# The conditioning vector of a Hymba block, spread over all partitions by eight transposes of one column each, and 24 warming matmuls where there were 31

## The chip, the cores and the metric

The kernel runs on one core of one Trainium2 chip. The metric is the device time of one execution in microseconds (us). Before the change it is 238.06 us, the median of three runs (237.94 to 239.41).

## The reference

One decoder layer for 512 tokens of width 1024, in float32. All of `x`, `c` and the weights are float32. Cut to what matters:

```python
c_act = jax.nn.silu(c)                                   # (1, 1024)
mod = c_act @ w_mod + b_mod                              # (1, 3072)
shift, scale, gate = jnp.split(mod, 3, axis=-1)
h = rmsnorm(x, norm_gain) * (1.0 + scale) + shift        # (512, 1024)
proj = h @ w_in                                          # (512, 3072)
q, k, v, z_attn, x_lru, z_lru = jnp.split(proj, splits, axis=-1)
attn = moba_attention(apply_rope(q), apply_rope(k), v)   # block-sparse causal, 8 heads x 64
y_attn = rmsnorm(attn, attn_out_gain) * silu(z_attn)
rec = rg_lru(causal_depthwise_conv(x_lru), ...)
y_lru = rmsnorm(rec, lru_out_gain) * silu(z_lru)
y = jnp.concatenate([y_attn, y_lru], axis=-1) @ w_out
return rmsnorm(x + gate * y, final_gain)
```

## The kernel before

`h` is kept transposed: eight tiles `h0` to `h7`, each of 128 channels by 512 tokens. Tile d is made from four transposes of normalised tokens (`xp`, line 412 for d >= 1, line 416 for d = 0, where they are issued one by one), and ScalarE applies the modulation to it as a scale and a bias per partition (line 419, `g`, twice: rounded as `h0h` and in full as `h`). Every matrix product is made of three passes over rounded halves (`h0h` and `h0l`, `w01h` and `w01l`, and so on): high by high, low by high, high by low. `split` (lines 233 and 251) makes the halves of a weight, the high one on ScalarE, the low one on VectorE.

The first phase accumulates seven column groups of the projection in seven PSUM banks (`acc`, line 431), d = 0 to 7, 21 matmuls of 512 columns for each d. For each d the modulation columns `shift` and `scale` have to be there: VectorE multiplies rows of the transposed `w_mod` (`ws`) by `cb`, which is SiLU(c) repeated on all 128 partitions, and sums along the row (line 384 for d = 0 in four pieces, line 396 after it). After that come the other columns, attention, the recurrence and the output product.

`cb` is made at the start. A small load brings `first`, 11 rows of 128: eight rows of c, then gain, shift and scale of d = 0. ScalarE takes SiLU of the eight rows (`crow`, line 320). TensorE turns `first` (line 325) so that VectorE can pick gain, shift and scale as columns (`v0`, line 326). Eight f32 products then spread `crow` (line 336): the stationary operand is one column of the identity repeated 128 times, over 8 rows, so each product repeats one row of `crow` on 128 partitions. They fill two banks `cp`, which are copied to `cb` (line 234).

TensorE's queue at the start also carries `NWARM` matmuls of 512 columns over a constant tile `warm` into a bank `spare` nobody reads (line 312).

The order of instructions on every engine comes from a planner (`Plan.emit`): each operation has a cost and a due time, the planner places the operation that can start first by its own model, and among those that can start within 0.12 us the one that is due first. The due times and costs are the numbers in `op(...)`. The engines execute their own queue in the order in which it was emitted. A load is issued on SyncE's queue (line 240).

Of the kernel before, what the change touches and what calls it, by code (L numbers as in the profile page):

```python
# [10 lines left out]
AF = mybir.ActivationFunctionType  # L11
OP = mybir.AluOpType
# [5 lines left out]
ND = D // 128  # L18
# [1 line left out]
BIG = 3.0e38  # L20
LRU_C = 8.0
NFIRST = 7
NWARM = 31
CUTS = (((0, 768), (768, 1024)), ((0, 512), (512, 1024)))
REST = (14.6, 14.7, 17.2, 17.3)

# [34 lines left out]
class Plan:  # L61
# [11 lines left out]
    def op(self, eng, cost, fn, r=(), w=(), due=None, table=None, lat=0.25, after=0.0, alt=None):  # L73
        o = Op(eng, cost, fn, list(r), list(w), due, table, lat, after, alt)
        deps = set()
        for b in o.r:
            if b.writer is not None:
                deps.add(b.writer)
        for b in o.w:
            if b.writer is not None:  # L80
                deps.add(b.writer)
            deps.update(b.readers)
        for b in o.r:
            b.readers.append(o)
        for b in o.w:
            b.writer, b.readers = o, []
        for b in set(o.r) | set(o.w):
            b.users += 1
        deps.discard(o)
        o.deps = list(deps)  # L90
        for d in deps:
            d.outs.append(o)
        o.left = len(deps)
        self.ops.append(o)
        return o
# [82 lines left out]
def tile_hymba_block(ctx: ExitStack, tc: tile.TileContext, x, ws0, wss, wgt, win0, wv, winr,  # L178
                     wo, wg, vecs, top, fgain, consts, out):
    nc = tc.nc  # L180
    V, A, G, PE, SP = nc.vector, nc.scalar, nc.gpsimd, nc.tensor, nc.sync
# [19 lines left out]
    op = plan.op  # L201
# [4 lines left out]
    def t4(name, dt=F32, shape=(128, 1024)):  # L206
        return Buf("t4", list(shape), dt, name)

    def bank(name, kind=None):
        return Buf("ps", [128, 512], F32, name, kind)  # L210

    def col(name):
        return Buf("c", [128, 2], F32, name)

    def fix(name, shape, dt=F32):
        return Buf("fix", list(shape), dt, name)


    def dv(n, ptr=0):
        return 0.075 + n / 960.0 + 0.06 * ptr  # L220
# [10 lines left out]
    def copy(n, dst, src, r, w, due=None, psum=False, after=0.0):  # L231

        op("A", acp(n) if psum else ac(n), lambda: A.copy(dst(), src()), r, w, due, after=after,  # L233
           alt=("V", dv(n) if psum else dv2(n), lambda: V.tensor_copy(dst(), src())))
# [27 lines left out]
    def t_first(d):  # L262
        return T_FIRST + 4.79 * d
# [10 lines left out]
    vec, ident, cst = fix("vec", [128, NV]), fix("ident", [128, 128]), fix("cst", [128, 2048])  # L274
    first = fix("first", [11, 128])
# [34 lines left out]
    op("V", 0.3, lambda: V.memset(warm[:], 1.0), [], [warm], -10)  # L310
    for n in range(NWARM):
        op("PE", 0.32 if n < 11 else 0.235, lambda: PE.matmul(spare[:], warm[:, 0:128], warm[:], start=True, stop=True),  # L312
           [warm], [spare], 5.3 + 0.28 * n, lat=0.0)


    epsc, ones, junk, crow = fix("epsc", [128, 1]), fix("ones", [128, 1]), fix("junk", [128, 1]), fix("crow", [ND, 128])
    op("V", 0.1, lambda: V.memset(epsc[:], EPS), [], [epsc], -20)
    op("V", 0.1, lambda: V.memset(ones[:], 1.0), [], [ones], 0)
    op("A", 0.1, lambda: A.activation(junk[:], epsc[:], AF.Silu), [epsc], [junk], -6, "silu")
    op("A", 0.1, lambda: A.activation(crow[:], first[0:ND, :], AF.Silu), [first, junk], [crow], -5, "silu")  # L320
    op("A", 0.1, lambda: A.activation(junk[:], epsc[:], AF.Sqrt), [epsc, crow], [junk], -4, "sqrt")


    ps, v0 = bank("v0"), fix("v0", [128, 3])
    op("PE", 0.2, lambda ps=ps: PE.transpose(ps[:, 0:11], first[:], ident[0:11, 0:11]), [first, ident], [ps], 1)
    op("V", 0.2, lambda ps=ps: (V.tensor_copy(v0[:, 0:2], ps[:, ND:ND + 2]), V.tensor_scalar(
        v0[:, 2:3], ps[:, ND + 2:ND + 3], 1.0, None, op0=OP.add)), [ps], [v0], 2)
    cb = t4("cb")
    for half in range(2):
        ps = bank("cp")  # L330
        s = slice(half * 512, (half + 1) * 512)

        def spread(ps=ps, half=half):
            for j in range(4):
                k = half * 4 + j
                PE.matmul(ps[:, j * 128:(j + 1) * 128], ident[0:ND, k:k + 1].to_broadcast([ND, 128]), crow[:], start=True, stop=True)  # L336
        op("PE", 0.8, spread, [crow, ident], [ps], 2)
        copy(512, lambda s=s: cb[:, s], lambda ps=ps: ps[:], [ps], [cb], 4.5 + 0.5 * half, True)


# [3 lines left out]
    for t in range(NT):  # L344
# [8 lines left out]
        for dst, cut, e, due2, after in ((xs[t], slice(0, 256), "VVAA"[t], due + 0.4, 0.0), (xt[t], slice(256, D), "A", 20.0 + t, REST[t])):  # L353
# [5 lines left out]
            else:  # L359
# [9 lines left out]
                                         op0=OP.add), [vec], [vec], t_first(1) - 3)  # L369

    sch = col("sch")

    def part(d, j):
        return ws[d][j][:, j] if d >= 4 else ws[d][j][:]

    def gain(d):

        sc, g = col("sc"), col("g")
        half = (sc, sch)
        for j in (1, 0):  # L380
            if d == 0:
                for n in range(2):
                    lo, up = CUTS[j][n]
                    op("V", dv(up - lo), lambda j=j, n=n, lo=lo, up=up: V.scalar_tensor_tensor(
                        ws[0][j][n][:], ws[0][j][n][:], 1.0, cb[:, lo:up], op0=OP.mult, op1=OP.mult,
                        accum_out=half[n][:, j:j + 1]), [ws[0][j][n], cb], [ws[0][j][n], half[n]], 8 - 2 * j + 0.7 * n)
                    if j and not n:
                        op("V", 0.1, lambda: V.tensor_add(sc[:, 1:2], sc[:, 1:2], v0[:, 2:3]), [sc, v0], [sc], 9.2)
                if j:
                    op("V", 0.2, lambda: V.tensor_scalar(g[:, 1:2], sch[:, 1:2], sc[:, 1:2], v0[:, 0:1],  # L390
                                                         op0=OP.add, op1=OP.mult), [sc, sch, v0], [g], 9.4)
                else:
                    op("V", 0.15, lambda: V.scalar_tensor_tensor(g[:, 0:1], sc[:, 0:1], v0[:, 1:2], sch[:, 0:1],
                                                                    op0=OP.add, op1=OP.add), [sc, sch, v0], [g], 9.5)
                continue
            op("V", dv(1024), lambda j=j: V.scalar_tensor_tensor(  # L396
                part(d, j), part(d, j), 1.0, cb[:], op0=OP.mult, op1=OP.mult, accum_out=sc[:, j:j + 1]),
               [ws[d][j], cb], [ws[d][j], sc])
        if d == 0:
            return g  # L400
        op("V", 0.2, lambda: V.tensor_scalar(
            g[:, 1:2], sc[:, 1:2], vec[:, V_SCALE + d:V_SCALE + d + 1], vec[:, V_GAIN + d:V_GAIN + d + 1],
            op0=OP.add, op1=OP.mult), [sc, vec], [g])
        op("V", 0.1, lambda: V.tensor_add(g[:, 0:1], sc[:, 0:1], vec[:, V_SHIFT + d:V_SHIFT + d + 1]), [sc, vec], [g])
        return g

    for d in range(ND):
        g, xp = gain(d), bank(f"xp{d}")
# [18 lines left out]
        for i, (a, b) in enumerate(((0, hh[d]), (1, hh[d]), (0, hl[d]))):  # L427
            for j in range(NFIRST):
                w, k = wp[j // 4][a], j if d else j % 4
# [293 lines left out]
    for u, name in enumerate(UNITS):  # L723
        kind, idx = name[0], int(name[1])
        t1 = t_step(8 * (u + 1))
        ps = unit(u)
# [41 lines left out]
    for g in range(4):  # L768
# [12 lines left out]
        for t in range(NT):  # L781
# [3 lines left out]
            for n, (lo, up) in enumerate(zip(cuts, cuts[1:])):  # L785
                ps, w = bank("po"), up - lo
# [39 lines left out]
                for to, up, mark in ((outa[t], 512, done_a), (outb[t], 512, done_b))[:1 if last else 2]:  # L826
                    fns = dict(A=lambda t=t, to=to, up=up: A.activation(to[:, :up], to[:, :up], AF.Copy, scale=ssq[t][:, 3:4]),
                               V=lambda t=t, to=to, up=up: V.tensor_scalar(to[:, :up], to[:, :up], ssq[t][:, 3:4], None, op0=OP.mult))
# [86 lines left out]
```

## Time and profile before

| | us |
|---|---|
| median of three runs | 238.06 |
| lowest and highest | 237.94, 239.41 |
| the profiled execution | 238.57 |
| its span, first to last instruction | 236.5 |
| TensorE busy in the span | 229.0 |
| VectorE busy | 203.8 |
| ScalarE busy | 139.3 |

The profile is of one execution; its times count from the first instruction. Engines: PE is TensorE's matmuls, PEld its weight loads, which overlap the matmuls, DVE is VectorE, ACT is ScalarE, SP is SyncE, which here only issues loads and stores. A busy share is an average over the program; which engine sets the end is read from the chain of work that ended last and from what each engine waited for.

### The profile page before, as it was taken

What the parts mean: (1) busy time and instruction counts of PE and PEld (TensorE: products, weight loads), DVE (VectorE), ACT (ScalarE), POOL (GpSimd) and SP (SyncE); (2) the same over time, 40 slices, a digit from 0 to 9 for tenths busy, and PEclk for the clock granted to TensorE, in tenths of its full rate; (3) what the DMA queues carried; (4) which work ended last, traced back from release to release, by engine and by line L of the source; (5) the groups of instructions that cost most, each with busy time, mean ns of one, the idle gap of its engine ahead of it and who ended that gap; (6) DMA issues with size and microseconds to landing.
All of it is one profiled execution on the core that took longest, in us unless ns stands there. A gap on an engine that the chain in (4) does not pass through costs nothing.

```text
span 236.5 us, 3435 instructions
## 1 busy us (share of the span) xinstructions
PE 229.0 (97%) x1236; PEld 181.2 (77%) x1236; DVE 203.8 (86%) x396; ACT 139.3 (59%) x263; POOL 9.5 (4%) x32
## 2 busy tenths in 40 slices
PE   7999999999999999999999999999999999999990
PEld 5457888888888788786788887878887788888890
DVE  1679998895999899899999999989998999956583
ACT  7859464652659587799992347766374711303363
POOL 1010000057000000000000000000000000000000
PEclk9999999999999999999999999999999999999997
DMA  6999999822045223755122354474521000000044
GB/s 232 378 418 417 416 418 423 327 91 89 11 169 177 89 89 103 256 191 167 61 118 89 92 190 180 166 256 190 177 89 65 26 0 3 0 0 0 0 180 177
DMA packets 11782, 38.54 MB, mean 163 GB/s; under 512 B 1515, under 2 KB 1782, under 8 KB 11638
## 3 DMA queue, kind: packets, MB, share of 16 engines
q1 hardware_dynamic: 11600, 38.06, 43.5%
q10 hardware_dynamic: 166, 0.27, 0.3%
q8 instruction: 10, 0.16, 0.3%
q14 instruction: 6, 0.05, 0.1%
HBM read 36.22 MB, written 2.10 MB: 162 GB/s over the span
## 4 chain that ended last, share of the span: by engine, by line
PE 96%; ACT 1%; DVE 1%; issue 0%
PE acc L431 17%; PE pj L243 14%; PE pj L245 13%; PE pj L244 13%; PE po L243 6%; PE po L245 6%; PE po L244 6%; PE spare L312 4%; PE av L616 4%; PE sc L570 4%; PE tp L633 4%; PE cp L336 2%; PE xp L412 1%; PE ss L758 1%; PE gi L243 0%; PE gi L245 0%
## 5 line engine op out<-in xcount | busy, mean ns | idle before, releaser
L586 ACT ACTIVATE z<-z,mn 128x128 f32<-128x128 f32 (+3 forms) x32 | 17.7, 554 | 7.9 <-DVE mn L583 7.2
L396 DVE SCALAR_TENSOR_TENSOR ws<-ws,cb 128x1024 f32<-128x1024 f32 x14 | 16.9, 1219 | 0.4 <-DMA ws<-in_wss_dram 0.4
L583 DVE CUSTOM_DVE_ANT_0 z<-sc,cst 128x128 f32<-128x128 f32 (+3 forms) x32 | 14.2, 487 | 1.6 <-PE sc L570 1.6
L233 ACT COPY pt<-tp 128x128 f32<-128x128 f32 (+3 forms) x26 | 8.5, 391 | 6.2 <-PE tp L633 6.2
L312 PE MATMUL spare<-warm 128*128 128x512 bf16 x31 | 10.2, 486 | 1.5 <-DVE warm L310 1.5
L796 DVE SCALAR_TENSOR_TENSOR xr<-po,rba,xr 128x512 f32<-128x512 f32 (+2 forms) x9 | 6.2, 692 | 6.2 <-PE po L245 6.0
L807 ACT ACTIVATE o<-xr 128x512 f32<-128x512 f32 x7 | 4.4, 635 | 12.0 <-DVE xr L796 12.0
L633 PE MATMUL tp<-ident,z 128*128 128x128 f32 x80 | 10.5, 272 | 0.0
L633 PEld LDWEIGHTS tp<-ident,z 128*128 128x128 f32 x80 | 9.4, 140 | 1.4
L778 DVE TENSOR_TENSOR wo<-wo,grow 128x1024 f32<-128x1024 f32 x8 | 9.8, 1219 | 0.0
L541 DVE SCALAR_TENSOR_TENSOR wgt<-wgt,cb 128x1024 f32<-128x1024 f32 x8 | 9.7, 1218 | 0.0
L495 DVE SCALAR_TENSOR_TENSOR xc<-xl,vec,xc 128x511 f32<-128x511 f32 (+2 forms) x12 | 9.0, 747 | 0.2
L616 PE MATMUL av<-pt,v 128*64 128x512 f32 (+3 forms) x64 | 9.1, 436 | 0.0
L312 PEld LDWEIGHTS <-warm 128*128 128x128 bf16 x31 | 3.5, 118 | 6.1 <-issue 2.9
L616 PEld LDWEIGHTS av<-pt,v 128*64 128x64 f32 x64 | 4.3, 137 | 5.0 <-issue 4.1
L598 DVE TENSOR_SCALAR z<-z,sum 128x384 f32<-128x384 f32 (+3 forms) x20 | 7.2, 387 | 0.4
L233 ACT CAST wo21h<-wo 128x1024 fp32r<-128x1024 f32 x1 | 1.1, 1054 | 9.7 <-DVE wo L778 9.7
L657 ACT ACTIVATE sz<-pj 128x512 f32<-128x512 f32 x8 | 4.8, 599 | 3.3 <-PE pj L245 2.8
L419 ACT ACTIVATE h<-xp,g 128x512 f32<-128x512 f32 x8 | 6.2, 771 | 0.0
L597 ACT ACTIVATE z<-z,sum 128x128 f32<-128x128 f32 (+3 forms) x12 | 6.2, 546 | 0.0
L796 DVE SCALAR_TENSOR_TENSOR xr<-po,rbl,xr 128x512 f32<-128x512 f32 x8 | 6.0, 747 | 0.2
L586 ACT ACTIVATION_READ_ACCUMULATOR z<-z,mn 128x1 f32 x32 | 6.0, 188 | 0.0
(1121 smaller groups left out, 753.5 us busy)
## 6 DMA issues: line engine op xcount, KB each, us to landing
wc<-in_winr_dram SPq DMA_DIRECT2D x13, 512.0 KB, 3.3
ws<-in_wss_dram SPq DMA_DIRECT2D x4, 1024.0 KB, 11.1
wgt<-in_wgt_dram SPq DMA_DIRECT2D x8, 512.0 KB, 3.3
wo<-in_wo_dram SPq DMA_DIRECT2D x8, 512.0 KB, 3.4
w<-in_win_dram SPq DMA_DIRECT2D x7, 448.0 KB, 8.8
ws<-in_wss_dram SPq DMA_DIRECT2D x6, 512.0 KB, 6.4
x<-in_x_dram SPq DMA_DIRECT2D x4, 512.0 KB, 5.4
wv<-in_wv_dram SPq DMA_DIRECT2D x4, 512.0 KB, 3.8
```

The costliest lines, as they stand in the source:

```text
L243: PE.matmul(ps, lh, rh, start=start, stop=False)
L244: PE.matmul(ps, lh, rl, start=False, stop=False)
L245: PE.matmul(ps, ll, rh, start=False, stop=stop)
L312: op("PE", 0.32 if n < 11 else 0.235, lambda: PE.matmul(spare[:], warm[:, 0:128], warm[:], start=True, stop=True), [warm], [spare], 5.3 + ...
L396: op("V", dv(1024), lambda j=j: V.scalar_tensor_tensor(part(d, j), part(d, j), 1.0, cb[:], op0=OP.mult, op1=OP.mult, accum_out=sc[:, j:j + ...
L431: PE.matmul(acc[j][:], w[:, k * 128:(k + 1) * 128], b[:], start=first, stop=last),
L583: op("V", dv(n) + 0.085, lambda s=s, z=z, mn=mn: V.tensor_tensor_reduce(out=z[:, :n], in0=ps[s][:, cut], in1=cst[:, 2048 - n:2048], op0=OP ...
L586: op("A", ac(n, 1, 1), lambda s=s, z=z, mn=mn, sm=sm: A.activation(z[:, :n], z[:, :n], AF.Exp, bias=mn[:, 0:1], scale=-1.0, accum_out=sm[: ...
L616: PE.matmul(pss[u][64 * s:64 * s + 64, k * 128:], vt[k][:, h * 64:h * 64 + 64], pts[2 * u + s][:, k, k * 128:], start=(k == 0), stop=(k == 3))
L633: PE.transpose(at(h)[:, k * 128:(k + 1) * 128], z[:, k * 128:(k + 1) * 128], ident[:])
L778: op("V", dv(1024), lambda w=w, s=s: V.tensor_mul(w[:], w[:], grow[:, None, s].to_broadcast([128, 2, 512])), [w, grow], [w], t0 - 7 + 2 * j)
L796: op("V", dv(w, 1), lambda t=t, ps=ps, c0=c0, c1=c1, br=br: V.scalar_tensor_tensor(res[t][:, c0:c1], ps[:, :c1 - c0], rb[br][:, t:t + 1], ...
```

## The change

SiLU is written back into `first`. The turn of `first` then carries the eight activated rows of c as well, all eleven columns are copied to `v0`, and eight transposes spread columns 0 to 7 of `v0`: the operand that is turned is one column repeated 128 times. The tile `crow` goes, the added 1 of the scale column gets a tile `one`, and the gain and shift columns of `v0` move behind the eight of c. `NWARM` becomes 24.

```diff
-NWARM = 31
+NWARM = 24
...
-    op("A", 0.1, lambda: A.activation(crow[:], first[0:ND, :], AF.Silu), [first, junk], [crow], -5, "silu")
-    op("A", 0.1, lambda: A.activation(junk[:], epsc[:], AF.Sqrt), [epsc, crow], [junk], -4, "sqrt")
+    op("A", 0.1, lambda: A.activation(first[0:ND, :], first[0:ND, :], AF.Silu), [first, junk], [first], -5, "silu")
+    op("A", 0.1, lambda: A.activation(junk[:], epsc[:], AF.Sqrt), [epsc, first], [junk], -4, "sqrt")
...
-    ps, v0 = bank("v0"), fix("v0", [128, 3])
-    op("PE", 0.2, lambda ps=ps: PE.transpose(ps[:, 0:11], first[:], ident[0:11, 0:11]), [first, ident], [ps], 1)
-    op("V", 0.2, lambda ps=ps: (V.tensor_copy(v0[:, 0:2], ps[:, ND:ND + 2]), V.tensor_scalar(
-        v0[:, 2:3], ps[:, ND + 2:ND + 3], 1.0, None, op0=OP.add)), [ps], [v0], 2)
+    ps, v0 = bank("v0"), fix("v0", [128, ND + 3])
+    op("PE", 0.3, lambda ps=ps: PE.transpose(ps[:, 0:ND + 3], first[:], ident[0:ND + 3, 0:ND + 3]), [first, ident], [ps], 1)
+    op("V", 0.15, lambda ps=ps: V.tensor_copy(v0[:], ps[:, 0:ND + 3]), [ps], [v0], 2)
+    one = fix("one", [128, 1])
+    op("V", 0.1, lambda: V.tensor_scalar(one[:], v0[:, ND + 2:ND + 3], 1.0, None, op0=OP.add), [v0], [one], 3)
...
-                PE.matmul(ps[:, j * 128:(j + 1) * 128], ident[0:ND, k:k + 1].to_broadcast([ND, 128]), crow[:], start=True, stop=True)
-        op("PE", 0.8, spread, [crow, ident], [ps], 2)
+                PE.transpose(ps[:, j * 128:(j + 1) * 128], v0[:, k:k + 1].to_broadcast([128, 128]), ident[:])
+        op("PE", 0.85, spread, [v0, ident], [ps], 2.5)
```

On TensorE, at the start of the program before the change: `v` is the turned `first`, `cp` the spread, `warm` and `spare` the warming matmuls.

```order
L312 LDWEIGHTS warm
L312 MATMUL spare<-warm 128x512
L325 MATMUL v_101<-ident,first 128x11
L336 MATMUL cp<-crow,ident 128x128 x8
L312 LDWEIGHTS warm
L312 MATMUL spare<-warm 128x512
```

The same place after the change:

```order
L312 LDWEIGHTS warm
L312 MATMUL spare<-warm 128x512
L325 MATMUL v_102<-ident,first 128x11
L312 LDWEIGHTS warm
L312 MATMUL spare<-warm 128x512
L312 LDWEIGHTS warm
L312 MATMUL spare<-warm 128x512
L337 MATMUL cp<-ident,v_105 128x128 x8
L312 LDWEIGHTS warm
L312 MATMUL spare<-warm 128x512
```

Ahead of the turn stand five warming matmuls where there were four, between the turn and the spread two where there was none, and between the spread and the first transpose of `xs` six where there were eight. Between the first and the second transpose of `xs` there are five where there were seven.

On TensorE, from the third transpose of `xs` (line 416 before, 417 after) to the first accumulation, before the change; behind the second transpose and ahead of the first row here stand nine warming matmuls:

```order
L416 MATMUL xp_145<-ident,xs_188 128x128
L312 LDWEIGHTS warm
L312 MATMUL spare<-warm 128x512
L312 LDWEIGHTS warm
L312 MATMUL spare<-warm 128x512
L312 LDWEIGHTS warm
L312 MATMUL spare<-warm 128x512
L416 MATMUL xp_145<-ident,xs_198 128x128
L412 MATMUL xp_208<-ident,xs_134 128x128
```

After the change, with six warming matmuls ahead of the first row that is shown as a transpose:

```order
L312 LDWEIGHTS warm
L312 MATMUL spare<-warm 128x512
L417 MATMUL xp_148<-ident,xs_186 128x128
L417 MATMUL xp_148<-ident,xs_193 128x128
L413 MATMUL xp_201<-ident,xs_138 128x128
L413 MATMUL xp_201<-ident,xs_157 128x128
```

The three warming matmuls between the last two transposes of `xs` are gone, and of the nine ahead of them six are left. On the other engines no instruction changes its place.

## Rows read from the trace of the kernel before

**Rows 1.** The page: busy time of each engine with its share of the span, and the chain of work that ended last, by engine.

```profile
PE 229.0 (97%) x1236; PEld 181.2 (77%) x1236; DVE 203.8 (86%) x396; ACT 139.3 (59%) x263; POOL 9.5 (4%) x32
PE 96%; ACT 1%; DVE 1%; issue 0%
```

**Rows 2.** The chain of work that ended last in order of time, 0 to 25 us: start, duration, engine, tile written, line, instructions merged.

```profile
3.63 3.61 PE cp L336 x16
7.24 3.52 PE spare L312 x8
10.77 0.21 PE xp L416
10.98 1.73 PE spare L312 x7
...
12.82 1.94 PE spare L312 x9
14.76 0.11 PE xp L416
14.87 0.65 PE spare L312 x3
...
15.66 0.79 ACT h0h L419
...
16.49 6.96 PE acc L431 x28
```

**Rows 3.** ScalarE's timeline, 10 to 22 us: start, duration, engine, line, operation, tile written and read, and in brackets the idle time before it and what ended it.

```profile
11.03 1.08 ACT L357 ACTIVATE xs<-x,ss 128x256 f32<-128x256 f32 x2
12.73 0.62 ACT L233 CAST w00512h<-w 128x512 fp32r<-128x512 f32 x1 [0.62 <-DMA w<-in_win_dram]
15.66 0.78 ACT L419 ACTIVATE h0h<-xp,g 128x512 fp32r<-128x512 f32 x1 [2.31 <-PE xp L416]
16.34 0.50 ACT L233 CAST w00384h<-w 128x384 fp32r<-128x384 f32 x1
...
19.07 0.93 ACT L233 CAST w01h<-w 128x896 fp32r<-128x896 f32 x1
...
20.74 0.77 ACT L419 ACTIVATE h1h<-xp,g 128x512 fp32r<-128x512 f32 x1
```

**Rows 4.** VectorE's timeline, 3 to 20 us, with the same columns.

```profile
3.67 0.16 DVE L326 COPY v<-v 128x2 f32<-128x2 f32 x1 [2.18 <-PE v L325]
...
7.28 0.69 DVE L234 COPY cb<-cp 128x512 f32<-128x512 f32 x1 [1.01 <-PE cp L336]
...
10.16 0.69 DVE L384 SCALAR_TENSOR_TENSOR ws<-ws,cb 128x512 f32<-128x512 f32 x1 [0.20 <-DMA ws<-in_ws_dram]
...
13.19 0.22 DVE L393 SCALAR_TENSOR_TENSOR g<-sc,v,sch 128x1 f32<-128x1 f32 x1
...
14.52 1.23 DVE L396 SCALAR_TENSOR_TENSOR ws<-ws,cb 128x1024 f32<-128x1024 f32 x1 [0.44 <-DMA ws<-in_wss_dram]
...
16.87 0.56 DVE L251 TENSOR_TENSOR w00384l<-w,w00384h 128x384 fp32r<-128x384 f32 x1 [1.12 <-ACT w00384h L233]
17.35 1.22 DVE L396 SCALAR_TENSOR_TENSOR ws<-ws,cb 128x1024 f32<-128x1024 f32 x1
...
18.49 0.69 DVE L421 TENSOR_TENSOR h0l<-h,h0h 128x512 fp32r<-128x512 f32 x1
...
19.50 0.15 DVE L404 TENSOR_TENSOR g<-sc,vec 128x1 f32<-128x1 f32 x1
```

**Rows 5.** Issues of single loads on SyncE's queue (duration of the issue in ns, smallest, median and largest, and first and last start in us) and the time from issue to landing: the two pieces of the weights of d = 0, the weights of d = 1 (`w01`), the second half of `ws` of d = 1.

```profile
L240 SPq DMA_DIRECT2D w<-in_win_dram x2: 527/797/1067, 4.6 to 5.7; - x2
DMA to landing us min/median/max: 7.5/7.8/8.1
L240 SPq DMA_DIRECT2D w<-in_win_dram x1: 328/328/328, 10.8 to 10.8; - x1
DMA to landing us min/median/max: 6.2/6.2/6.2
L240 SPq DMA_DIRECT2D ws<-in_wss_dram x1: 327/327/327, 10.2 to 10.2; - x1
DMA to landing us min/median/max: 5.7/5.7/5.7
```

**Rows 6.** TensorE's timeline, 16.4 to 22 us: the first products of `h0l` and of `h1h`.

```profile
16.49 1.21 PE L431 MATMUL acc<-h0h,w00512h 128*128 128x512 f32 x4 [0.43 <-ACT h0h L419]
...
19.83 1.07 PE L431 MATMUL acc<-h0l,w00512h 128*128 128x512 f32 x4
...
21.56 0.73 PE L431 MATMUL acc<-h1h,w01h 128*128 128x512 f32 x2
```

**Rows 7.** Who waited for whom: the only two rows of TensorE's matmuls over the whole program, then one of ScalarE from 14 to 62 us (us in total, times, longest).

```profile
PE spare L312 <- DVE warm L310: 1.5, 1, 1.5
PE acc L431 <- ACT h0h L419: 0.4, 1, 0.4
ACT h3h L419 <- PE xp L412: 2.5, 1, 2.5
```

**Rows 8.** The chain in order of time, one row of 176 to 182 us (`tp` are transposes of the attention), and the last 3.3 us of the span by stretch: length, busy time and instructions of PE, PEld, DVE, ACT and POOL, the granted clock as a share of 2.4 GHz, DMA share and GB/s.

```profile
177.80 1.75 PE tp L633 x16
233.20:236.50 3.30, 0.00 (x0) 0.00 (x0) 0.00 (x0) 0.00 (x0) 0.00 (x0) 0.50 0.46 176
```

More of the change, by code (lines that the diff above doesn't have):

```diff
@@ L313, in tile_hymba_block @@
            [warm], [spare], 5.3 + 0.28 * n, lat=0.0)
-    epsc, ones, junk, crow = fix("epsc", [128, 1]), fix("ones", [128, 1]), fix("junk", [128, 1]), fix("crow", [ND, 128])
+    epsc, ones, junk = fix("epsc", [128, 1]), fix("ones", [128, 1]), fix("junk", [128, 1])
     op("V", 0.1, lambda: V.memset(epsc[:], EPS), [], [epsc], -20)
@@ L387, in gain @@
                     if j and not n:
-                        op("V", 0.1, lambda: V.tensor_add(sc[:, 1:2], sc[:, 1:2], v0[:, 2:3]), [sc, v0], [sc], 9.2)
+                        op("V", 0.1, lambda: V.tensor_add(sc[:, 1:2], sc[:, 1:2], one[:]), [sc, one], [sc], 9.2)
                 if j:
-                    op("V", 0.2, lambda: V.tensor_scalar(g[:, 1:2], sch[:, 1:2], sc[:, 1:2], v0[:, 0:1],
+                    op("V", 0.2, lambda: V.tensor_scalar(g[:, 1:2], sch[:, 1:2], sc[:, 1:2], v0[:, ND:ND + 1],
                                                          op0=OP.add, op1=OP.mult), [sc, sch, v0], [g], 9.4)
                 else:
-                    op("V", 0.15, lambda: V.scalar_tensor_tensor(g[:, 0:1], sc[:, 0:1], v0[:, 1:2], sch[:, 0:1],
+                    op("V", 0.15, lambda: V.scalar_tensor_tensor(g[:, 0:1], sc[:, 0:1], v0[:, ND + 1:ND + 2], sch[:, 0:1],
                                                                     op0=OP.add, op1=OP.add), [sc, sch, v0], [g], 9.5)
```

## Prediction

> **What bounds the kernel now.** I read the totals first. TensorE is busy for 229.0 of 236.5 us, and the chain of work that ended last runs over it for 96% of the span [rows 1], so a change counts only if it lets TensorE reach its useful matmuls sooner or do fewer of them. Then the chain in order of time. Up to 15.6 us it names nothing but TensorE, and none of that is a product of the layer: 16 passes of the eight `cp` products, then 8, 7, 9 and 3 warming matmuls with the four transposes of `xs` between them [rows 2]. The first accumulation starts at 16.49 and from there the chain is TensorE again. The list of waits says that this stays so: over the whole program TensorE's matmuls wait twice, 1.5 us for `warm` at the start and 0.4 us for `h0h` [rows 7]. So the end of the kernel follows the start of the accumulations, d = 0 at 16.49 and d = 1 at 21.56 [rows 6].
>
> What does the first one wait for? In ScalarE's timeline `h0h` starts at 15.66 after 2.31 us of idle time that ended with a transpose of `xs` on TensorE [rows 3]. Its other inputs were there earlier: `g` is written at 13.19 + 0.22 = 13.41 [rows 4], and both late `xs` tiles by 11.03 + 1.08 = 12.11 [rows 3]. TensorE works strictly in its order, and the transposes of those two tiles stood behind nine and three warming matmuls. That is 2.2 us in which everything else was ready.
>
> **The clock in these rows.** Eight warming matmuls of 512 columns take 3.52 us from 7.24 (0.44 each, the 1.2 GHz level), nine take 1.94 from 12.82 (0.215 each, the 2.4 GHz level). The seven from 10.98 take 1.73, which is one slow and six fast: the clock rose near 11.4 [rows 2]. A transpose of 128 columns takes 0.21 before and 0.11 after [rows 2].
>
> **Part 1, the spreading of c.** Removed: eight f32 products, 3.61 us on TensorE [rows 2]. Added: eight transposes. At the low clock I take the 0.21 of the transpose at 10.77 for each, 1.7 us in all. Nothing shows a transpose whose stationary operand is one column repeated; the bound above is the price of the removed product, 3.61 / 8 = 0.45 each, the bound below the fast 0.11. I stay with 0.21, the row of the same operation at the same clock. Three more warming matmuls now stand ahead (one before the turn of `first`, two behind it), 3 x 0.44 = 1.3. So the last `cp` ends at 7.24 + 1.3 - 3.6 + 1.7 = 6.6 instead of 7.24.
>
> The change adds a wait: the transposes need `v0`, which VectorE copies out of PSUM after the turn; the same copy took 0.16 us from 3.67 [rows 4]. Behind the waiting transposes stand all the warming matmuls and the `xs` transposes. The two warming matmuls between turn and spread, 0.88 us, cover the copy; without that cover it would cost some 0.3. Who needs the result is `cb`, whose second half is copied at 7.28 and would now be at some 6.7; its first reader starts only at 10.16, and waited for a DMA then [rows 4]. Even at the upper bound (`cp` ending at 8.5, `cb` at 9.3) this reader sees nothing. So part 1 by itself is worth nothing at VectorE; what it gives is 0.6 us of TensorE's queue. The other edits (SiLU in place, one wider copy instead of two small ones, the added one in a tile of its own) are single short instructions with margin of the same kind, and I cost them at nothing.
>
> **Part 2, seven warming matmuls fewer.** The order shows where: none remains behind the second `xs` transpose but six, and none between the third and the fourth. From 6.6: six at 0.44 end at 9.3, the first `xs` transpose at 9.5, five more (four of them slow, if the clock again rises near 11.4) at 11.55, the second transpose at 11.65, six fast ones at 12.95, the last two transposes at 13.2. They need `xs` of 12.11, so they wait for nothing. `h0h` then starts at the latest of 13.2 (transposes), 13.41 (`g`) and the end of the `w00512h` cast, 12.73 + 0.62 = 13.35 [rows 3], so near 13.45: **2.2 us** sooner. If the clock rises 2 us later than that, some 1.3 us come on top for TensorE and `h0h` starts near 14.5.
>
> **What is late next.** Each engine's queue behind `h0h` has to come 2.2 sooner too, or it gives back time.
> - ScalarE: the cast of `w00384h` follows `h0h` by 0.68, so 14.13; its load landed 7.5 to 8.1 after issues at 4.6 and 5.7 [rows 5], 13.2 at the latest. No stall.
> - VectorE: `w00384l` waited 1.12 for that cast [rows 4]. This wait goes, but not more: the reduction ahead of it began at 14.5, when its load came. So everything behind it on VectorE moves by 1.12 and not by 2.2: the next reduction from 17.35 to 16.23 (its load, issued at 10.2, landed 5.7 later at 15.9 [rows 5], just in time), and `h0l` from 18.49 to 17.37, ready at 18.06.
> - TensorE: the 14 products of `h0h` take 19.83 - 16.49 = 3.34 [rows 6]. From 14.27 they end at 17.6, and the products of `h0l` wait for 18.1. That is **0.45 given back**. The seven `h0l` products then take 1.6 (0.23 each, as 6.96 / 28 less the start [rows 2]) and end at 19.7.
> - d = 1: `h1h` needs `g`, which moves by 1.12 from 19.65 to 18.53 [rows 4], and ScalarE, where the cast of `w01h` moves from 19.07 to 17.0: there the load stops it, issued at 10.8 and landed 6.2 later [rows 3, 5]. Everything behind it moves by 2.07, so `h1h` starts at 18.67 and ends at 19.45, before TensorE is free at 19.7. Before, TensorE had waited about 0.1 for it.
>
> So d = 1 starts at 19.7 to 19.8 instead of 21.56: 2.2 - 0.45 + 0.1 = **1.8 us sooner**. Behind that TensorE is dense, and the others wait for it: already `h3h` stood 2.5 us for TensorE's transposes [rows 7], more than the 1.8. I find nothing that returns the 1.8.
>
> **The sum.** The profiled execution took 238.57 us, its span 236.5 and 2.1 around it; that is 0.5 over the median of 238.06. It becomes 238.57 - 1.8 = 236.8, and by the same difference the median becomes **236.3 us**, a ratio of 0.992. About 1% (2.4 us) is what a measurement of this kernel tells from no change, so the likeliest outcome lies inside it.
>
> **Rivals.**
> *The clock falls in the new gap.* In the stretch from 12.95 to 14.27 TensorE would have six transposes and then nothing, where before it had a 1 us stretch of that kind. Price: at 0.44 a product instead of 0.23, a clock that stays low for T us from 14.27 delays d = 1 by 0.47 T. The wait for `h0l` hides the first 0.45 of that and the 1.8 goes next, so from T = 2.25 / 0.47, about 5 us, on the kernel is slower than before; low through all of d = 0 (21 x 0.43 = 9 us) puts d = 1 at 23.3, 1.7 later than now: 239.8. Against it: 16 transposes alone from 177.80 took 1.75 us, 0.109 each, so the clock stood high through them; for it: it is at 0.50 in the last stretch, where TensorE has nothing at all [rows 8]. The Trainium skill (TensorE: Matmul & The Clock Gate, Part 4: PE-mode transpose) says that the full clock "doesn't engage for transpose-mode"; by that the six transposes would not count against this rival, and its 239.8 would be the sum. The row at 177.80 differs from the page: transposes there ran at the full clock and alone for longer than this gap, so the chance stays small. 0.07.
>
> *The loads become the bound.* `w01` has 0.1 us of margin and the second reduction 0.4. Every us that these land later than in this trace is a us less gained: 0.6 to 1.2 later gives 237 to 237.5. 0.15.
>
> *The change does not do what it says.* If `g` rather than the warming matmuls had set `h0h` in most executions, or the spread came after 10.16, nothing would move: 238.1. The 2.31 us row speaks against the first, a margin of 2.8 us against the second. 0.05.
>
> *More than forecast.* The kernel before carries some 18 warming matmuls behind the rise of its clock; where it rises 1 us later than in this trace, two more run slow and `h0h` comes 0.5 later. If that is the usual case the gain is 2.3 or more: 235.7. 0.10.
>
> **How the numbers follow.** The forecast has 0.63, with 235.9 to 236.8 as its own range (0.1 to 0.5 us for the landings, and as much for the clock's moment). The range of 8 in 10 leaves out the falling clock and the lower part of the last rival, 0.12 or so, and with the edges of the forecast not above 2 in 10; it takes in the late loads and no change, with 0.1 for the spread of a median: 235.4 to 238.2. Faster by over 1% (below 235.7) is only the better half of the last rival and the edge of the forecast: 0.09. Slower by over 1% needs a clock that stays low into d = 1, 10.5 us: 0.04. Within 1%: 0.87.
>
> **What would show it.** Right: `h0h` starts near 13.45 after a wait for `g`, not for TensorE; eight `cp` transposes of 0.21; TensorE waits about 0.4 for `h0l`; d = 1 starts near 19.75, and the span ends 1.8 sooner with everything behind d = 1 unchanged in spacing. Wrong: products of `h0h` 0.43 apart instead of 0.23 (clock), an idle stretch of ScalarE ahead of `w01h` that ended with a DMA (loads), or `h0h` still behind `xs` transposes.

## The result, and the profile after

| | before | after |
|---|---|---|
| median of 20 runs, us | 238.57 | 236.77 |
| lowest and highest | 237.84, 239.44 | 235.79, 239.01 |
| profiled execution, its span | 238.57, 236.5 | 237.26, 235.2 |
| d = 1 starts in the profile | 21.56 | 20.38 |

The ratio is 0.9929 with a 95% interval of 0.991 to 0.9948: 1.8 us faster, the size that was forecast, inside the 1% that was named. The profile after shows that this number came about in another way than the working said.

TensorE's timeline after, 4 to 21 us, with the columns of [rows 6]:

```profile
4.82 1.91 PE L337 MATMUL cp<-ident,v 128*128 128x128 f32 x8
6.53 1.77 PE L312 MATMUL spare<-warm 128*128 128x512 bf16 x6
...
8.25 1.24 PE L312 MATMUL spare<-warm 128*128 128x512 bf16 x5
...
9.43 1.46 PE L312 MATMUL spare<-warm 128*128 128x512 bf16 x6
...
11.70 0.33 PE L417 MATMUL xp<-ident,xs 128*128 128x128 f32 x1 [0.36 <-ACT xs L358]
...
13.88 2.00 PE L432 MATMUL acc<-h0h,w00512h 128*128 128x512 f32 x4 [1.41 <-ACT h0h L420]
15.68 1.49 PE L432 MATMUL acc<-h0h,w00384h 128*128 128x512 f32 x3
16.95 1.30 PE L432 MATMUL acc<-h0h,w00512l 128*128 128x512 f32 x4
...
18.79 1.07 PE L432 MATMUL acc<-h0l,w00512h 128*128 128x512 f32 x4
...
20.38 0.84 PE L432 MATMUL acc<-h1h,w01h 128*128 128x512 f32 x3
```

The eight transposes of the spread start at 4.82 and the next matmul at 6.53, 0.21 each. Of the six warming matmuls behind them the most, and all behind those, run at 0.215: the clock rose near 7 us, where before it rose near 11.4 [rows 2]. The trace's own record of the granted clock begins with this rise, at 7.15 us after and at 11.30 before. The clock column of a stretch (third from the end, with the columns of [rows 8]) counts nothing ahead of the record and reads 1.00 there, as in this stretch of the profile before, in which the warming matmuls take 0.44. So ahead of the first rise the level is read from the spacing of the matmuls.

```profile
5.90:11.80 5.90, 5.90 (x20) 2.95 (x19) 3.67 (x14) 4.83 (x12) 0.00 (x0) 1.00 1.00 377
```

After the change TensorE is therefore through with its 24 warming matmuls at 11 us, waits 0.36 us for `xs`, and after the transposes stands empty for 1.41 us until `h0h` is there. Then the first seven products of `h0h` are 0.45 and 0.42 apart instead of 0.23: the clock has fallen. By the trace's record it is at 0.50 from 13.98 to 17.39. Stretches of the profile after, with the same columns:

```profile
14.20:16.80 2.60, 2.60 (x7) 2.04 (x7) 2.60 (x4) 2.42 (x5) 1.08 (x1) 0.50 1.03 408
17.50:20.00 2.50, 2.50 (x13) 2.04 (x12) 2.46 (x6) 2.50 (x5) 0.00 (x0) 1.00 1.02 406
```

ScalarE's timeline after, which answers [rows 3]:

```profile
12.37 0.62 ACT L233 CAST w00512h<-w 128x512 fp32r<-128x512 f32 x1 [0.72 <-DMA w<-in_win_dram]
13.05 0.78 ACT L420 ACTIVATE h0h<-xp,g 128x512 fp32r<-128x512 f32 x1
13.73 0.50 ACT L233 CAST w00384h<-w 128x384 fp32r<-128x384 f32 x1
...
16.73 0.94 ACT L233 CAST w01h<-w 128x896 fp32r<-128x896 f32 x1 [0.18 <-DMA w<-in_win_dram]
...
18.42 0.76 ACT L420 ACTIVATE h1h<-xp,g 128x512 fp32r<-128x512 f32 x1
```

`h0h` starts 2.6 us sooner and directly behind the cast of `w00512h`, whose load ends the wait; the transposes of `xs` no longer hold it. VectorE's first reduction waits for a DMA, as before, and it has `h0l` at 16.96 + 0.69:

```profile
9.66 0.69 DVE L385 SCALAR_TENSOR_TENSOR ws<-ws,cb 128x512 f32<-128x512 f32 x1 [0.26 <-DMA ws<-in_ws_dram]
...
12.73 0.22 DVE L394 SCALAR_TENSOR_TENSOR g<-sc,v,sch 128x1 f32<-128x1 f32 x1
...
16.96 0.69 DVE L422 TENSOR_TENSOR h0l<-h,h0h 128x512 fp32r<-128x512 f32 x1
```

TensorE reaches the products of `h0l` only at 18.79, a us after that, since it runs slowly; d = 1 starts 1.2 us sooner than before, and the span ends 1.3 sooner. This profile is not the usual case. The other runs have no trace, but each has its mean granted clock, and a fall of 3.4 us to half takes 0.007 from the mean over 235 us. In 8 of the 20 runs the mean is 0.983 to 0.988 (0.987 in the profiled one) and the time 237.1 to 239.0, median 237.5; in the other 12 it is 0.991 to 0.998 and the time 235.8 to 237.0, median 236.5. That the first group are the runs in which the clock fell is read from these means. The means also hold a low stretch at the end of the span, which every profile has, so a single run near the border could be misplaced. The median of all lies within the faster group.

### The profile page after: what moved, and what is told of

Same layout as the page of the kernel before. It is cut to its first block, busy times and chain, and to the rows that moved or that the text cites. A ratio compares the mean times of both kernels' runs of the same rounds, so it can differ in the third digit from the quotient of the medians.

```text
span 235.2 us, 3405 instructions
## 1 busy us (share of the span) xinstructions
PE 226.1 (96%) x1221; PEld 179.7 (76%) x1221; DVE 203.9 (87%) x396; ACT 139.7 (59%) x263; POOL 9.5 (4%) x32
## 4 chain that ended last, share of the span: by engine, by line
PE 91%; DMA 3%; SPq 2%; ACT 1%; DVE 1%; issue 0%; ACTq 0%
PE acc L432 17%; PE pj L243 14%; PE pj L245 13%; PE pj L244 13%; PE po L243 6%; PE po L245 6%; PE po L244 6%; PE av L617 4%; PE sc L571 4%; PE tp L634 4%; DMA w<-in_win_dram 3%; SPq L240 2%; PE xp L413 1%; PE ss L759 1%; PE gi L245 0%; PE gi L243 0%
## 5 line engine op out<-in xcount | busy, mean ns | idle before, releaser
L312 PE MATMUL spare<-warm 128*128 128x512 bf16 x24 | 7.7, 466 | 1.5 <-DVE ones L318 1.5
L312 PEld LDWEIGHTS <-warm 128*128 128x128 bf16 x24 | 2.5, 114 | 4.1 <-DVE ones L318 1.5
```

## The experiments

The theory after the profile: products over 8 rows had kept TensorE's clock low; with the transposes it rises some 4 us sooner, that by itself sets `h0h` free, and the seven missing warming matmuls then leave TensorE empty, so that the clock falls in part of the runs. The rival is the prediction's own working: the clock rises when it did, part 1 is worth 0.6 us of queue, and the gain is that of part 2. All medians below are compared with the kernel before on the same chip: 239.02 us (17 runs) for e1 to e4, 239.01 (16 runs) for e5 and e6.

**e1: part 1 alone.** The changed kernel with

```diff
-NWARM = 24
+NWARM = 31
```

> Part 1 alone: the spread by eight transposes, 31 warming matmuls. Theory (from the profile after): with transposes in place of the products over 8 rows the clock rises near 7 us and not near 11.4, so the 18 warming matmuls behind the spread run at 0.215 and the last xs transpose comes at 12.2 to 12.5; h0h starts at 13.0 to 13.5, held by g and the w00512h cast, and TensorE is not empty before it, so the clock does not fall. Time about 1.7 us below before, ratio 0.992 to 0.994. Rival (the prediction's own working): the clock rises near 11.4 as before and part 1 gives 0.6 us of TensorE's queue; h0h near 15.0, ratio 0.997 to 0.998.

Measured: 236.06 us, six runs from 235.62 to 236.16, ratio 0.9885 (0.9862 to 0.9908). The gain of part 1 alone, 3.0 us, is larger than the theory said and larger than that of the whole change. TensorE's timeline:

```profile
6.52 1.88 PE L312 MATMUL spare<-warm 128*128 128x512 bf16 x6
...
9.54 2.10 PE L312 MATMUL spare<-warm 128*128 128x512 bf16 x9
...
12.23 0.27 PE L417 MATMUL xp<-ident,xs 128*128 128x128 f32 x1
...
13.57 1.19 PE L432 MATMUL acc<-h0h,w00512h 128*128 128x512 f32 x4 [0.41 <-ACT h0h L420]
14.60 0.84 PE L432 MATMUL acc<-h0h,w00384h 128*128 128x512 f32 x3
15.28 1.07 PE L432 MATMUL acc<-h0h,w00512l 128*128 128x512 f32 x4
...
17.43 1.19 PE L432 MATMUL acc<-h0l,w00512h 128*128 128x512 f32 x4 [0.40 <-DVE h0l L422]
...
19.15 0.86 PE L432 MATMUL acc<-h1h,w01h 128*128 128x512 f32 x3
```

The nine warming matmuls and the three behind them are there (part 2 takes six of these twelve away), but they run at 0.215, and the last transpose of `xs` comes at 12.23 and not, as in the profile before, at 15.35:

```profile
15.35 0.27 PE L416 MATMUL xp<-ident,xs 128*128 128x128 f32 x1
```

The clock rose at 7.36 by the trace's record. ScalarE starts `h0h` at 12.74, behind the cast, as in the changed kernel:

```profile
12.09 0.62 ACT L233 CAST w00512h<-w 128x512 fp32r<-128x512 f32 x1 [0.74 <-DMA w<-in_win_dram]
12.74 0.78 ACT L420 ACTIVATE h0h<-xp,g 128x512 fp32r<-128x512 f32 x1
```

TensorE waits 0.41 for it, and its first seven products come out 0.26 and 0.23 apart. The rival's clock near 11.4 and its ratio of 0.997 fall. Part of why the gain is larger than the theory said is the load behind the cast: the cast starts at 12.09 where it started at 12.73 before. Over the eight profiles of this case that start lies between 11.56 (e5) and 12.90 (e4, the changed kernel again), and no run shows whether the change has a share in it. The wait of 0.40 for `h0l` is the 0.45 that the prediction gave back.

**e2: part 2 alone.** The kernel before with

```diff
-NWARM = 31
+NWARM = 24
```

> Part 2 alone: the f32 products over 8 rows, 24 warming matmuls. Theory: the products keep the clock low, it rises near 11 us, the seven missing warming matmuls let the xs transposes end near 14.1, h0h starts near 14.15, 1.5 us sooner than before; TensorE is never empty, so the clock stays high; h0l again takes some back, ratio 0.993 to 0.995. Rival: the gain of the whole change comes from the spread alone and the count of warming matmuls does nothing: ratio 0.998 to 1.002.

Measured: 237.51 us, 12 runs from 236.84 to 239.12, ratio 0.995 (0.993 to 0.9969), 1.5 us. TensorE's timeline:

```profile
7.25 3.59 PE L312 MATMUL spare<-warm 128*128 128x512 bf16 x8
...
10.84 1.76 PE L312 MATMUL spare<-warm 128*128 128x512 bf16 x7
...
13.63 0.38 PE L416 MATMUL xp<-ident,xs 128*128 128x128 f32 x2
...
14.88 1.21 PE L431 MATMUL acc<-h0h,w00512h 128*128 128x512 f32 x4 [0.43 <-ACT h0h L419]
...
19.95 0.97 PE L431 MATMUL acc<-h1h,w01h 128*128 128x512 f32 x3
```

With the products over 8 rows the clock again rises only near 11 (eight at 0.42 from 7.25, then seven in 1.6; 11.02 by the trace's record), and `h0h` starts at 14.05, 1.6 us sooner than before:

```profile
14.05 0.78 ACT L419 ACTIVATE h0h<-xp,g 128x512 fp32r<-128x512 f32 x1 [0.74 <-DVE w00512l L251]
```

The view puts this wait down to a subtraction on VectorE that is no input of `h0h`; the last two transposes of `xs`, which are, end at the same time (13.63 + 0.38). So here the warming matmuls do stand in the way, as the working had it. TensorE is never empty for longer than 0.43 before the products of `h0h`, and the clock holds. The two parts do not add: 3.0 and 1.5 alone, 2.3 together (e4).

**e3: the gap filled.** The changed kernel with six more warming matmuls behind the fourth transpose of `xs`; the order of everything else is the same.

```diff
+NHOLD = 6
...
+        for n in range(NHOLD if not d else 0):
+            op("PE", 0.235, lambda: PE.matmul(spare[:], warm[:, 0:128], warm[:], start=True, stop=True),
+               [warm, xs[3]], [spare], 11.0 + 0.01 * n, lat=0.0)
```

> The changed kernel with six more warming matmuls behind the fourth xs transpose, where TensorE had been empty for 1.4 us before the products of h0h. Theory: the clock no longer falls during d = 0, products of h0h are 0.23 apart, every run is as fast as those of the changed kernel in which the clock held; span 234.0 to 234.7, median 0.3 to 0.6 us below the changed kernel, ratio 0.989 to 0.991. Rival: the low stretch costs nothing, since h0l waits anyway, and the runs spread for another reason: ratio 0.992 to 0.994, the same as the changed kernel.

Measured: 236.09 us, six runs from 235.64 to 236.69, ratio 0.9891 (0.9869 to 0.9913), and mean clocks of 0.991 to 0.998 in all of them. TensorE's timeline, then the stretch at the products of `h0h`:

```profile
11.56 1.46 PE L421 MATMUL spare<-warm 128*128 128x512 bf16 x6
...
13.57 1.19 PE L436 MATMUL acc<-h0h,w00512h 128*128 128x512 f32 x4
...
19.14 0.86 PE L436 MATMUL acc<-h1h,w01h 128*128 128x512 f32 x3
```

```profile
14.20:16.80 2.60, 2.60 (x13) 2.01 (x11) 2.60 (x6) 2.42 (x4) 1.01 (x1) 1.00 1.03 411
```

Thirteen matmul records in the stretch in which the changed kernel has seven, at the full clock. With work added that nobody reads, the median is 0.6 us below that of the changed kernel on the same chip (e4), and the times above 237 are gone. The intervals of e3 and e4 overlap, so the 0.6 by itself is not clear of noise; what speaks for the fillers is that the 12 runs of e1 and e3 have no mean below 0.991, where 11 of the 26 runs of the changed kernel (8 of 20 above, 3 of 6 in e4) have 0.988 or less.

**e4: the changed kernel again**, without an edit.

> The changed kernel again, for a second profile and its times beside the three others on the same chip. Ratio 0.992 to 0.994. If the clock holds in this profile: h0h near 13.1 to 13.5, TensorE waits 0.3 to 0.5 us for h0l, d = 1 starts near 19.7, span near 234.5. If it falls: d = 1 near 20.4, span near 235.2.

Measured: 236.68 us, six runs from 235.85 to 237.72, ratio 0.9917 (0.9888 to 0.9946). The clock fell in three of the six (mean 0.986 to 0.988; 237.2 to 237.7) and held in three (0.991 to 0.996; 235.9 to 236.2). The profile is again one in which it fell, this time with everything half a us later, and d = 1 at 20.88. A profile of the changed kernel with the clock held is therefore missing; e1 and e3 stand in for it.

**e5: the same products over 128 rows.** The kernel before, all 31 warming matmuls; `crow` is padded with 120 rows of zeros, the products are otherwise the same.

```diff
-    epsc, ones, junk, crow = fix("epsc", [128, 1]), fix("ones", [128, 1]), fix("junk", [128, 1]), fix("crow", [ND, 128])
+    epsc, ones, junk, crow = fix("epsc", [128, 1]), fix("ones", [128, 1]), fix("junk", [128, 1]), fix("crow", [128, 128])
...
-    op("A", 0.1, lambda: A.activation(crow[:], first[0:ND, :], AF.Silu), [first, junk], [crow], -5, "silu")
+    op("V", 0.1, lambda: V.memset(crow[:], 0.0), [], [crow], -15)
+    op("A", 0.1, lambda: A.activation(crow[0:ND, :], first[0:ND, :], AF.Silu), [first, junk, crow], [crow], -5, "silu")
...
-                PE.matmul(ps[:, j * 128:(j + 1) * 128], ident[0:ND, k:k + 1].to_broadcast([ND, 128]), crow[:], start=True, stop=True)
+                PE.matmul(ps[:, j * 128:(j + 1) * 128], ident[:, k:k + 1].to_broadcast([128, 128]), crow[:], start=True, stop=True)
```

> The kernel before with one thing changed: the same eight f32 products, but over 128 rows (crow padded with zero rows) in place of 8. They take as long as before (0.45 each, 3.6 us in all). Theory: it was the products over 8 rows that kept the clock low until 11.3; over 128 rows the clock rises near 7 to 8 us, the warming matmuls behind them run at 0.215, the last xs transpose comes near 13.4 and h0h near 13.5, with no transposes in the spread and all 31 warming matmuls; time 236.2 to 236.8, ratio 0.989 to 0.993. Rival: f32 products keep the clock low whatever their rows, or the early rise comes from the transposes themselves: the clock rises near 11.3 and the time is that of before, ratio 0.998 to 1.002.

Measured: 236.34 us, six runs from 236.05 to 236.7, ratio 0.9889 (0.9865 to 0.9912). One warming matmul moved, from ahead of the first transpose of `xs` to behind the last. TensorE's timeline:

```profile
3.70 3.63 PE L337 MATMUL cp<-crow,ident 128*128 128x128 f32 x16
7.17 1.67 PE L312 MATMUL spare<-warm 128*128 128x512 bf16 x7
8.68 0.27 PE L417 MATMUL xp<-ident,xs 128*128 128x128 f32 x1
...
13.11 0.27 PE L417 MATMUL xp<-ident,xs 128*128 128x128 f32 x1
...
14.25 1.19 PE L432 MATMUL acc<-h0h,w00512h 128*128 128x512 f32 x4 [0.22 <-ACT h0h L420]
...
19.32 0.96 PE L432 MATMUL acc<-h1h,w01h 128*128 128x512 f32 x3
```

The products take the 3.6 us that they took over 8 rows, TensorE's queue holds as much as before, and the spread has no transpose in it. But the warming matmuls behind them run at 0.215 from the first one on, where over 8 rows eight took 0.44 each [rows 2]; the clock rose at 7.04 by the trace's record, and 2.7 us are gained. The slowest of the six runs is 1.2 us below the fastest of the 16 of the kernel before (237.93). So neither a shorter spread nor transposes are needed for most of the gain of e1; it is enough that the products over 8 rows are no longer there while the clock is to rise.

**e6: 18 warming matmuls.** The changed kernel with

```diff
-NWARM = 24
+NWARM = 18
```

> The changed kernel with 18 warming matmuls: the six between the second and the third xs transpose are gone too, so TensorE is empty from about 9.8 to the products of h0h near 13.5 but for the transposes. h0h cannot start sooner than with 24, since g and the w00512h cast hold it. Theory: the clock is low during d = 0 in more of the runs, or for longer; 237.0 to 238.2, slower than the changed kernel, mean granted clock 0.983 to 0.988 in most runs. Rival: the clock has nothing to do with the warming matmuls in this gap: the same time as the changed kernel, 236.5 to 236.9, with the same share of runs at the lower mean clock.

Measured: 237.73 us, 12 runs from 236.58 to 238.94, ratio 0.995 (0.9927 to 0.9973); mean clocks of 0.981 to 0.988 in all 12. TensorE's timeline, then two stretches:

```profile
11.31 0.33 PE L417 MATMUL xp<-ident,xs 128*128 128x128 f32 x1 [2.22 <-ACT xs L358]
...
14.12 2.08 PE L432 MATMUL acc<-h0h,w00512h 128*128 128x512 f32 x4 [0.85 <-ACT h0h L420]
...
17.27 1.80 PE L432 MATMUL acc<-h0h,w00512l 128*128 128x512 f32 x4
...
21.21 0.84 PE L432 MATMUL acc<-h1h,w01h 128*128 128x512 f32 x3
```

```profile
11.30:12.80 1.50, 1.18 (x5) 1.00 (x6) 1.46 (x6) 0.70 (x2) 0.00 (x0) 0.73 1.06 412
14.20:16.80 2.60, 2.60 (x6) 2.08 (x7) 2.36 (x4) 2.60 (x4) 1.08 (x1) 0.50 1.04 413
```

By their means the clock falls in all 12 runs when the gap is longer. In the profile it falls sooner (11.98) and stays low for longer, 6.8 us where it was 3.4. But in this execution it also rose sooner, at 5.16 by the trace's record, where the other four profiles with the transposes have 7.15 to 7.84 behind the same work. So the earlier moment of the fall is not shown to come from the longer gap; that it falls every time is. ScalarE starts `h0h` at 13.29, still directly behind the cast, so nothing was there to be won by fewer warming matmuls. The median is 1.05 us above that of e4; the intervals of the two ratios overlap, so the size of the loss is not settled. The rival wanted the same share of runs at the lower mean clock; it was 3 of 6 and is 12 of 12, so the rival falls.

## Why the prediction came true, and where its working failed

- **The bound** was read rightly. The end follows the start of d = 1: from before to e1 that start moved by 2.4 us and the span by 2.6 (236.5 to 233.9), from before to after by 1.2 and 1.3.
- **The price of a transpose**, 0.21 at the low clock, was right, and so was that the wait for `v0` is hidden: VectorE's products with `cb` start at 9.66, after a DMA, as before.
- **The step that failed** is one half sentence in part 2, "if the clock again rises near 11.4". It carried a time over from the trace of before although part 1 takes away the very work that TensorE did until then. The clock rose near 7. The account of where the gain comes from was wrong by this: part 1 was costed at 0.6 us of queue and gives 3.0 alone (e1); most of the 2.2 at `h0h` was laid to part 2, which is worth 1.5 alone (e2) and beside part 1 wins nothing (the median without it, e1, is 0.6 lower than with it, e4, with intervals that overlap). And with the early clock TensorE is done sooner than the working said, so that the gap opens in which the clock can fall.
- **`h0h`** was to start at 13.45, held by `g` or the cast; it starts at 13.05 behind the cast. The limit was right; the load came 0.4 sooner in this execution. This limit is why the wrong time of the rise did not spoil the sum: the transposes were to end at 13.2, with `g` and the cast near 13.4, and they end at about 12.5, with `g` and the cast near 13.0. Neither way do they set `h0h`.
- **The 0.45 given back at `h0l`** was right where the clock holds: 0.40 in e1. The stall of `w01h` on its load is there too, 0.18.
- **The rival with the falling clock** had the right mechanism, and its chance, 0.07, was far too small: 8 of 20 runs, 3 of 6 in e4. The sign that was named for it, products of `h0h` 0.43 apart, is in the profile. It was weighed for a gap of 1.3 us with six transposes in it. The row put against it, 16 transposes from 177.80, shows a clock that stays up through transposes directly behind other products; no empty stretch followed them, so it said little on this gap. With the clock up since 7 TensorE was short of work from 11 us on. Its price held: 0.47 of the 3.4 us of low clock, less the 0.45 that the wait for `h0l` hides, is 1.15; measured are 0.9 (d = 1 at 20.38 against 19.15 in e1, of which 0.31 is the later `h0h`). So does its limit: with 3.4 us, under the 5 us that were named, the run stays faster than before.
- **The sum** of 1.8 was met so closely by luck: where the clock holds, the gain is 2.0 (236.5 against 238.57), 0.2 more than forecast, and the runs in which it falls, which were given almost no weight, take the 0.2 back from the median. On the chip of the experiments the same change gave 2.3 (e4).
- The level was 0.5 off, 236.77 for 236.3, since the median of 20 runs of before is 238.57 where three runs gave 238.06. Why runs of the kernel before spread over 1.6 us was not tried. A fall of the clock like the one above does not explain it: of its 33 runs beside the experiments those up to 238.40 have means of 0.991 to 0.992, and those from 238.68 on, the slower ones, have 0.993 to 0.995.

Three kernels here have a lower median than the changed one on the same chip (236.68): the changed one with 31 warming matmuls (236.06), the one with six behind the last transpose of `xs` (236.09) and the kernel before with the products over 128 rows (236.34). Their intervals overlap with that of the changed kernel; all are clear of the kernel before.

## What to carry to other kernels

Whoever changes what TensorE does while its clock is to rise has moved the rise itself; a time of the clock read from the old trace must not stand in the new sum. Nor is one new trace enough for it: with the same work ahead of the rise it came between 5.16 and 7.84 in five profiles. Filler that keeps the clock up is to be sized to the wait that it covers after the change, and a gap that opens ahead of dense work can cost more than filler that is a little too long: the changed kernel had the clock low in 11 of 26 runs by its means, and in none of the 12 with the gap filled (e1, e3). Where a profile shows one case, the clock means of the other runs tell how often it is the case.

## What the hardware did that was not expected

The same f32 products, 0.45 us each, left TensorE at the 1.2 GHz level when they used 8 rows (the eight warming matmuls behind them at 0.44, the rise at 11.30 before and 11.02 in e2) and did not over 128 rows (seven at 0.215 from the start, the rise at 7.04 in e5); rows of zeros were enough. And 1.4 us of an empty TensorE, behind a stretch with little but transposes, let the clock fall just as the real products began (13.98, and 14.66 in e4), by the means in 11 of 26 runs of the same kernel; with 2.2 us more of emptiness ahead of the transposes (e6) it fell in all 12.
